# Encoder trunk: gate and up as seven quarter products per pair of tiles

## Chip, core and metric

The kernel runs on one core of one Trainium2 chip. The metric is the device time of one execution in microseconds, the median of several runs. Inside the program the engines run side by side, each with its own queue of instructions in order: TensorE (PE, with its weight loads PEld), VectorE (DVE), ScalarE (ACT), GpSimd (POOL), and SyncE (SP), which only issues transfers. They wait for each other through semaphores.

## What is computed

Two layers of an encoder trunk on 512 tokens of width 1024. Each layer has two feed-forward blocks, an attention mix of three branches, and a gated embedding. Cut to what matters here:

```python
def swiglu(x, w_gate, w_up, w_down):          # w_gate, w_up: 1024 x 2816, w_down: 2816 x 1024
    return (jax.nn.silu(x @ w_gate) * (x @ w_up)) @ w_down

for i in range(DEPTH):                        # DEPTH = 2
    h = h + 0.5 * swiglu(rms_norm(h, ffn1_norm[i]), ffn1_w_gate[i], ffn1_w_up[i], ffn1_w_down[i])
    ...                                       # three attention branches, merged through w_out
    h = h + 0.5 * swiglu(rms_norm(h, ffn2_norm[i]), ffn2_w_gate[i], ffn2_w_up[i], ffn2_w_down[i])
    h = h + jax.nn.sigmoid(rms_norm(h, ple_norm[i]) @ ple_w_gate[i]) * (p[i] @ ple_w_proj[i])
```

## The kernel before

The activations lie transposed: `h[d]` is a tile of 128 model rows by 512 tokens, d = 0 to 7. Everything is float32. A product is made exactly enough by splitting each operand into a rounded part `hi` (type fp32r) and the remainder `lo`, and adding three matmuls, hi x hi, lo x hi, hi x lo (`mm3`). Each matmul has a weight load of its own of 128x128.

The weights come from one DRAM tensor, `wall`, cut into chunks of 128 x 1024 in the order of use. `Weights.load` (L64) brings a chunk into `wraw` (four buffers) by a transfer on SP; `Weights.halve` makes `whi` on ACT (L75) and `wlo` on DVE, in the attention heads on POOL (L76), with three buffers each.

A feed-forward block is the function `ffn`. `Prep` has made the input parts `z[d]` (gain times `h[d]`, hi on ACT L328, lo on DVE L329); the norm's factor `rb` is applied after the product. For each of the 22 tiles `f` of 128 hidden rows: 24 matmuls for gate, 24 for up, each 512 tokens wide, then four operations on DVE and ACT and a split into `a[f]` (L175, L176). `down(g)` takes the hidden tiles of a group (two tiles, then five times four) through w_down: 8 output tiles, each added to `h[d]` on DVE (L371). It is written between the tiles `f`, one tile after the group is whole. `hooks` add small work after a given `f`: the bias tables of the first layer (`bias_vectors`, after f = 8) end in 24 transfers on POOL's queue (L253).

`mix` is the attention: 40 heads, whose matmuls are interleaved by a planner (`Filler`, with due times) with the projections that they need. All its 512-wide tiles, as those of `ffn`, come from one pool of `SLOTS` = 79 buffers (function `S`). `w_out` and `add_out` end it; `ple` is the embedding.

The program is written with tiles; a scheduler sets the order on each engine ahead of the run, so an instruction may stand earlier on its engine than the source has it if its inputs are there. Within an engine the order is then fixed.

```python
            else:
                run(proj(pg, W.get(gate), z))
                run(proj(pu, W.get(up), z))
            g1, u1 = S(f"{name}g1_{f}"), S(f"{name}u1_{f}")
            nc.vector.tensor_mul(g1, pg, rb)
            nc.scalar.activation(g1, g1, AF.Silu)
            nc.vector.tensor_mul(u1, pu, rb)
            nc.vector.tensor_mul(u1, u1, g1)
            a[f] = split(u1, f"{name}a{f}")
```

## Time and profile before

| | |
|---|---|
| median of 3 runs | 3021.95 us (3021.86 to 3022.31) |
| profiled execution: its time | 3021.52 us |
| its span, first to last instruction | 3019.7 us |
| granted TensorE clock | 0.998 |
| feed-forward blocks in the span, first to last matmul | 9.7 to 375.7, 1103.2 to 1463.3, 1507.5 to 1868.7, 2598.2 to 2958.3 us |

The span is 1.8 us shorter than the profiled execution's time. Sums are made against the span. A group of instructions is given by line, engine, operation and the tiles that it writes and reads (`out<-in`), with its count, busy time and mean duration. The duration of a matmul is a modelled end; the distance from start to start says what a row of matmuls costs. Tile names in the trace: `ffn20g` is the gate product of the second block of layer 0, `f_0` its input norm and `z` parts, `m0vc` the values of the third branch in layer 0.

### The profile page before, as it was taken

What the parts mean: (1) busy time and instruction counts of PE and PEld (TensorE: products, weight loads), DVE (VectorE), ACT (ScalarE), POOL (GpSimd) and SP (SyncE); (2) the same over time, 40 slices, a digit from 0 to 9 for tenths busy, and PEclk for the clock granted to TensorE, in tenths of its full rate; (3) what the DMA queues carried; (4) which work ended last, traced back from release to release, by engine and by line L of the source; (5) the groups of instructions that cost most, each with busy time, mean ns of one, the idle gap of its engine ahead of it and who ended that gap; (6) DMA issues with size and microseconds to landing.
All of it is one profiled execution on the core that took longest, in us unless ns stands there. A gap on an engine that the chain in (4) does not pass through costs nothing.

```text
span 3019.7 us, 37502 instructions
## 1 busy us (share of the span) xinstructions
PE 2966.6 (98%) x14206; PEld 2463.6 (82%) x14206; DVE 1837.0 (61%) x2844; ACT 1418.5 (47%) x2511; POOL 749.0 (25%) x709
## 2 busy tenths in 40 slices
PE   8999999999999999999999999999999999999998
PEld 7888878888878888888888888788888788888886
DVE  6444576646787765444664445866478877644446
ACT  4222356655677742223432223566467777422233
POOL 0010015444455530000200001144344555200003
PEclk9999999999999999999999999999999999999999
DMA  4363332122222233333333334211222222333332
GB/s 154 99 221 98 122 126 70 49 70 73 77 77 79 76 116 98 97 93 97 125 103 95 96 98 158 83 63 57 63 82 74 68 75 75 124 95 96 98 98 91
DMA packets 81525, 287.75 MB, mean 95 GB/s; under 512 B 10382, under 2 KB 12430, under 8 KB 81344
## 3 DMA queue, kind: packets, MB, share of 16 engines
q1 hardware_dynamic: 66960, 240.42, 25.5%
q0 software_dynamic: 12080, 42.00, 4.1%
q10 hardware_dynamic: 2304, 2.94, 0.3%
q8 instruction: 111, 1.82, 0.2%
q14 instruction: 70, 0.57, 0.1%
HBM read 274.76 MB, written 18.94 MB: 97 GB/s over the span
## 4 chain that ended last, share of the span: by engine, by line
PE 88%; DVE 6%; ACT 4%; issue 2%; POOL 0%; DMA 0%; ACTq 0%; DVEq 0%; POOLq 0%
PE ffn10g L165 4%; PE ffn10u L165 4%; PE ffn21g L165 4%; PE ffn20g L165 4%; PE ffn21u L165 4%; PE ffn20u L165 4%; PE ffn21d L165 4%; PE ffn11d L165 4%; PE ffn10d L165 4%; PE ffn20d L165 4%; PE ffn11g L165 4%; PE ffn11u L165 4%; PE wo L165 3%; PE ple L165 3%; PE m1ga L165 1%
## 5 line engine op out<-in xcount | busy, mean ns | idle before, releaser
L75 ACT CAST whi<-wraw 128x1024 fp32r<-128x1024 f32 x456 | 478.4, 1052 | 1057.0 <-issue 371.3
L76 DVE TENSOR_TENSOR wlo<-wraw,whi 128x1024 fp32r<-128x1024 f32 x312 | 383.6, 1232 | 124.3 <-ACT whi L75 124.0
L76 POOL TENSOR_TENSOR wlo<-wraw,whi 128x1024 fp32r<-128x1024 f32 x144 | 353.4, 2457 | 366.5 <-ACT whi L75 322.0
L287 POOL TENSOR_TENSOR pg0sq<-pg0sq,pg0sq 128x512 f32<-128x512 f32 x7 | 11.1, 1586 | 345.0 <-ACT pg0sq L282 345.0
L287 POOL TENSOR_TENSOR pg1sq<-pg1sq,pg1sq 128x512 f32<-128x512 f32 x7 | 11.1, 1583 | 345.1 <-ACT pg1sq L282 345.1
L419 POOL DMA_DIRECT2D h_dram<-wo0h x8 | 4.3, 541 | 341.2 <-DVE wo0h L371 341.2
L371 DVE SCALAR_TENSOR_TENSOR wo0h<-ffn11d,wo0h 128x512 f32<-128x512 f32 x48 | 32.8, 689 | 40.9 <-PE ffn11d L165 40.9
L371 DVE SCALAR_TENSOR_TENSOR x<-ffn10d,x 128x512 f32<-128x512 f32 x48 | 32.8, 689 | 40.9 <-PE ffn10d L165 40.9
L371 DVE SCALAR_TENSOR_TENSOR wo1h<-ffn21d,wo1h 128x512 f32<-128x512 f32 x48 | 32.8, 689 | 38.7 <-PE ffn21d L165 38.7
L371 DVE SCALAR_TENSOR_TENSOR wo0h<-ffn20d,wo0h 128x512 f32<-128x512 f32 x48 | 32.8, 689 | 38.7 <-PE ffn20d L165 38.7
L388 DVE TENSOR_TENSOR ffn20u<-ffn20u,f_0r 128x512 f32<-128x512 f32 x22 | 15.2, 691 | 62.0 <-PE ffn20u L165 62.0
L388 DVE TENSOR_TENSOR ffn21u<-ffn21u,f_1r 128x512 f32<-128x512 f32 x22 | 15.2, 691 | 62.0 <-PE ffn21u L165 62.0
L388 DVE TENSOR_TENSOR ffn10u<-ffn10u,f_0r 128x512 f32<-128x512 f32 x22 | 15.2, 691 | 59.8 <-PE ffn10u L165 59.8
L419 POOL DMA_DIRECT2D h_dram<-x x8 | 4.3, 540 | 189.1 <-DVE x L371 189.1
L388 DVE TENSOR_TENSOR ffn11u<-ffn11u,f_1r 128x512 f32<-128x512 f32 x22 | 15.2, 691 | 59.2 <-PE ffn11u L165 59.2
L386 DVE TENSOR_TENSOR ffn21g<-ffn21g,f_1r 128x512 f32<-128x512 f32 x22 | 15.2, 691 | 47.0 <-PE ffn21g L165 46.9
L386 DVE TENSOR_TENSOR ffn20g<-ffn20g,f_0r 128x512 f32<-128x512 f32 x22 | 15.2, 691 | 47.0 <-PE ffn20g L165 46.9
L386 DVE TENSOR_TENSOR ffn10g<-ffn10g,f_0r 128x512 f32<-128x512 f32 x22 | 15.2, 691 | 44.5 <-PE ffn10g L165 44.4
L386 DVE TENSOR_TENSOR ffn11g<-ffn11g,f_1r 128x512 f32<-128x512 f32 x22 | 15.2, 690 | 44.1 <-PE ffn11g L165 44.1
L248 POOL DMA_DIRECT2D bias_s<-bvs x1 | 0.5, 519 | 142.5 <-DVE bvs L246 142.5
L287 POOL TENSOR_TENSOR f_1sq<-f_1sq,f_1sq 128x512 f32<-128x512 f32 x14 | 21.0, 1500 | 58.5 <-ACT f_1sq L282 58.3
L598 ACT CAST m0kc<-m0kc 64x512 fp32r<-64x512 f32 x32 | 18.6, 580 | 13.7 <-PE m0kc L165 6.1
(5072 smaller groups left out, 10383.7 us busy)
## 6 DMA issues: line engine op xcount, KB each, us to landing
wraw<-in_wall SPq DMA_DIRECT2D x456, 512.0 KB, 3.5
copies_s<-bias_s POOLq DMA_DIRECT2D x16, 256.0 KB, 7.7
copies_d<-bias_d POOLq DMA_DIRECT2D x8, 512.0 KB, 15.1
h_dram<-x POOLq DMA_DIRECT2D x8, 256.0 KB, 2.7
pp_dram<-m0ppt POOLq DMA_DIRECT2D x8, 256.0 KB, 4.7
wo0h<-h_dram POOLq DMA_DIRECT2D x8, 256.0 KB, 5.3
ple0p<-pp_dram POOLq DMA_DIRECT2D x8, 256.0 KB, 4.9
h_dram<-wo0h POOLq DMA_DIRECT2D x8, 256.0 KB, 2.7
```

What stands on the lines that cost most here:

```text
L75: self.nc.scalar.copy(hi, raw)
L76: self.lo_engine.tensor_tensor(lo, raw, hi.bitcast(F32), op=ALU.subtract)
L165: nc.tensor.matmul(ps, lhsT, rhs, start=start, stop=stop, skip_group_check=True)
L248: nc.gpsimd.dma_start(bias_s, bv[0:n, :])
L287: self.engine.tensor_tensor(self.acc, self.acc, sq, op=ALU.add)
L371: nc.vector.scalar_tensor_tensor(h[d], ps, 0.5, h[d], op0=ALU.mult, op1=ALU.add)
L386: nc.vector.tensor_mul(g1, pg, rb)
L388: nc.vector.tensor_mul(u1, pu, rb)
L419: nc.gpsimd.dma_start(h_dram[d], h[d])
L598: nc.scalar.copy(ks[e][r], ps[own])
```

## The change

From the second pair of hidden tiles on (p = 1 to 10 of 11), gate and up of a pair are each computed as a 2x2 block product: the two hidden tiles give two blocks of weight columns, the 1024 model rows two blocks of 512, and the 512 tokens two halves of 256 (`A`, `B`). Instead of eight quarter products there are seven, of four `mm3` each, 256 tokens wide, after the scheme of Strassen and Winograd.

- `Combos` makes the four sums of input quarters from `h`, once per block, in the time of the first pair, which is still done the plain way.
- `Quad` is one pair's gate or up. Its weights are two chunks, loaded on SP into `X` and `Y`, and half of the second again into `Z`. Two of the four sums of weights are made by transfers that add to their destination (on POOL's queue, `accum_op`), one by POOL and one by DVE (`took`).
- Two PSUM tiles, `R` and `V`, hold the partial products; copies on ACT and sums on DVE form the two results `t1`, `t2`. The last product (4) of a pair is done within the next pair.
- The factor `rb` enters through the gate: after Silu, POOL multiplies it in again, so that up needs no factor.
- Splitting into hi and lo goes by halves of 512 columns; two halves share a tile pair. A fourth tile pair is in a pool of its own.
- The steps of a block stand in a list, and `prepare` runs splits ahead of them by `AHEAD` tiles, loads by `LOADS` steps. `down` groups follow pairs 1, 3, 5, 7; the last two groups come at the end.
- Memory: the common pool has 62 buffers. The space of the other 17 and of the strips is a pool that is opened for each stage: weights' tiles in the feed-forward blocks, 17 tiles (`kept`) and the strips in `mix`.
- The second half of `w_out` goes column by column, so that `h[4]` to `h[7]` are done one after the other. The number of matmuls is the same.

```diff
+PAIRS = FT // 2
+DOWN_AFTER = {1: 0, 3: 1, 5: 2, 7: 3}
...
+    def tiles(self, stage=None):
+        n = self.pairs
+        self.pairs += 1
+        if stage is not None and n % 4 == 3:
+            return tuple(stage.tile([P, 1024], F32R, tag=f"w{x}2", name=f"w{x}{n}", bufs=1) for x in ("hi", "lo"))
+        return tuple(self.pool.tile([P, 1024], F32R, tag=f"w{x}", name=f"w{x}{n}", bufs=3) for x in ("hi", "lo"))
+    def part(self, hi, lo, raw):
+        self.nc.scalar.copy(hi, raw)
+        self.lo_engine.tensor_tensor(lo, raw, hi.bitcast(F32), op=ALU.subtract)
...
+    def open_stage(for_weights):
+        guard = tc.tile_pool(name=f"stage{len(stages)}", bufs=1, reuse_waits="tile")
+        pool = guard.__enter__()
+        stages.append(guard)
+        W.stage = pool if for_weights else None
+        return pool
...
+    class Combos(Prep):
+        def quarters(self):
+            A, B = HALVES
+            z = self.z
+            self.q = {1: [[t[:, A] for t in z[k]] for k in range(4)], 2: [[t[:, A] for t in z[4 + k]] for k in range(4)],
+                      3: [[t[:, B] for t in z[4 + k]] for k in range(4)], 4: [None] * 4, 5: [None] * 4, 6: [None] * 4, 7: [None] * 4}
+        def combine(self, k):
+            A, B = HALVES
+            name, one, two = self.name, self.at + k, self.at + 4 + k
+            zf = S(f"{name}zf{k}")
+            nc.scalar.activation(zf, h[k], AF.Copy, scale=col(self.l, one))
+            first, second = S(f"{name}t57{k}"), S(f"{name}t64{k}")
+            gain, other = col(self.l, two), ncol(self.l, two)
+            lo, hi = h[4 + k][:, A], h[4 + k][:, B]
+            nc.vector.tensor_sub(first[:, A], zf[:, A], zf[:, B])
+            nc.vector.scalar_tensor_tensor(second[:, A], hi, other, first[:, A], op0=ALU.mult, op1=ALU.subtract)
+            nc.vector.scalar_tensor_tensor(first[:, B], hi, gain, zf[:, B], op0=ALU.mult, op1=ALU.subtract)
+            nc.vector.scalar_tensor_tensor(second[:, B], lo, other, second[:, A], op0=ALU.mult, op1=ALU.subtract)
+            for t, nm, ops in ((first, "t57", (5, 7)), (second, "t64", (6, 4))):
+                parts = split(t, f"{name}{nm}{k}")
+                for i, c in zip(ops, HALVES):
+                    self.q[i][k] = [x[:, c] for x in parts]
...
+        def load(self):
+            L, R = slice(0, 512), slice(512, 1024)
+            n, m = self.places
+            stage, wall = W.stage, ins["wall"]
+            if self.weight.endswith("gate"):
+                X = stage.tile([P, 1024], F32, tag="wx", name=f"{self.name}x", bufs=2)
+            else:
+                X = wpool.tile([P, 1024], F32, tag="wraw", name=f"{self.name}x", bufs=4)
+            Y = stage.tile([P, 1024], F32, tag="wy", name=f"{self.name}y", bufs=4)
+            Z = stage.tile([P, 512], F32, tag="wz", name=f"{self.name}z", bufs=4)
+            nc.sync.dma_start(Y, wall[m])
+            nc.sync.dma_start(X, wall[n])
+            nc.sync.dma_start(Z, wall[m][:, L])
+            nc.gpsimd.dma_start(Y[:, L], wall[m][:, R], accum_op=ALU.add)
+            nc.gpsimd.dma_start(Z, wall[n][:, L], accum_op=ALU.add)
+            self.X, self.Y = X, Y
+            self.source = {1: X[:, L], 2: X[:, R], 5: Y[:, L], 6: X[:, L], 3: X[:, R], 7: Z, 4: Y[:, R]}
+        def took(self, i):
+            L, R = slice(0, 512), slice(512, 1024)
+            if i == 1:
+                nc.gpsimd.tensor_tensor(self.X[:, L], self.X[:, L], self.Y[:, L], op=ALU.add)
+            elif i == 2:
+                nc.vector.tensor_add(self.X[:, R], self.X[:, R], self.X[:, L])
+        def product(self, i, w):
+            A, B = HALVES
+            if i == 1:
+                self.R = PS(f"{self.name}R", "s")[:, A]
+                self.t = S(f"{self.name}t1"), S(f"{self.name}t2")
+            elif i == 2:
+                self.V = PS(f"{self.name}V", "a")
+            ps = {2: lambda: self.V[:, A], 5: lambda: self.V[:, B], 3: lambda: self.V[:, B]}.get(i, lambda: self.R)()
+            wh, wl = w
+            for k in range(4):
+                c = slice(k * P, (k + 1) * P)
+                zh, zl = self.combos.q[i][k]
+                mm3(ps, wh[:, c], wl[:, c], zh, zl, i in (1, 2) and k == 0, i in (4, 3) and k == 3)
+            t1, t2 = self.t
+            if i == 1:
+                nc.scalar.copy(t1[:, A], self.R)
+            elif i == 5:
+                nc.scalar.copy(t2[:, A], self.V[:, B])
+            elif i == 6:
+                nc.scalar.copy(t1[:, B], self.R)
+            elif i == 3:
+                nc.vector.tensor_add(t1, self.V, t1)
+            elif i == 7:
+                nc.vector.tensor_add(t2[:, B], self.R, t2[:, A])
...
+        def plain_pair():
+            for f in range(2):
+                pg, pu = PS(f"{name}g{f}"), PS(f"{name}u{f}")
+                gate, up = ("cols", tag + "_w_gate", l, f), ("cols", tag + "_w_up", l, f)
+                if f == 0:
+                    together((pg, pu), W.get(gate, up), prep.z)
+                    rstd()
+                    prep.quarters()
+                else:
+                    run(proj(pg, W.get(gate), prep.z))
+                    run(proj(pu, W.get(up), prep.z))
+                g1, u1 = S(f"{name}g1_{f}"), S(f"{name}u1_{f}")
+                nc.vector.tensor_mul(g1, pg, rb[0])
+                nc.scalar.activation(g1, g1, AF.Silu)
+                nc.vector.tensor_mul(u1, pu, rb[0])
+                nc.vector.tensor_mul(u1, u1, g1)
+                a[f] = split(u1, f"{name}a{f}")
+                for k in (2 * f, 2 * f + 1):
+                    prep.combine(k)
...
-                run(proj(pg, W.get(gate), z))
-                run(proj(pu, W.get(up), z))
-            g1, u1 = S(f"{name}g1_{f}"), S(f"{name}u1_{f}")
-            nc.vector.tensor_mul(g1, pg, rb)
-            nc.scalar.activation(g1, g1, AF.Silu)
-            nc.vector.tensor_mul(u1, pu, rb)
-            nc.vector.tensor_mul(u1, u1, g1)
-            a[f] = split(u1, f"{name}a{f}")
-            for g, fs in enumerate(GROUPS[:-2]):
-                if f == fs[-1] + 1:
-                    down(g)
-            if f in hooks:
-                hooks[f]()
-        root_table()
...
+        def gate_half(q, n):
+            t, r = q.t[n], rb[0]
+            if n == 0:
+                nc.vector.tensor_mul(t, t, r)
             else:
+                nc.vector.scalar_tensor_tensor(t[:, B], t[:, B], -1.0, r[:, B], op0=ALU.mult, op1=ALU.mult)
+                nc.vector.scalar_tensor_tensor(t[:, A], q.R, -1.0, r[:, A], op0=ALU.mult, op1=ALU.mult)
+            nc.scalar.activation(t, t, AF.Silu)
+            nc.gpsimd.tensor_tensor(t, t, r, op=ALU.mult)
+        def up_half(q, gq, n, f):
+            t, g = q.t[n], gq.t[n]
+            if n == 0:
+                nc.vector.tensor_mul(t, t, g)
+            else:
+                nc.vector.scalar_tensor_tensor(t[:, B], t[:, B], -1.0, g[:, B], op0=ALU.mult, op1=ALU.mult)
+                nc.vector.scalar_tensor_tensor(t[:, A], q.R, -1.0, g[:, A], op0=ALU.mult, op1=ALU.mult)
+            a[f] = split(t, f"{name}a{f}")
+        def product(q, i, then=lambda: None):
+            def do(w):
+                q.product(i, w)
+                then()
+            steps.append(("product", (q, i), do))
+        tail = []
+        for p in range(1, PAIRS):
+            G, U = [Quad(f"{name}{x}{p}", tag + "_w_" + w, p, prep) for x, w in (("g", "gate"), ("u", "up"))]
+            for i in (1, 2):
+                product(G, i)
+                product(U, i)
+            for fn in tail:
+                fn()
+            for i in (5, 6, 3, 7):
+                product(G, i, (lambda G=G: gate_half(G, 0)) if i == 3 else lambda: None)
+                product(U, i, (lambda G=G, U=U, p=p: up_half(U, G, 0, 2 * p)) if i == 3 else lambda: None)
+            tail = [lambda G=G: product(G, 4, lambda: gate_half(G, 1)),
+                    lambda G=G, U=U, p=p: product(U, 4, lambda: up_half(U, G, 1, 2 * p + 1))]
+            if p in DOWN_AFTER:
+                down(DOWN_AFTER[p])
+        at = len(steps)
         down(len(GROUPS) - 2)
+        for k, fn in enumerate(tail):
+            fn()
+            steps.insert(at + 2 + k, steps.pop())
         down(len(GROUPS) - 1, True)
+        plain_pair()
...
+        def load_upto(n):
+            while state["loaded"] < min(n, len(steps)):
+                kind, what, _ = steps[state["loaded"]]
+                if kind == "down":
+                    W.load(base[what] + 1)
+                elif what[0].source is None:
+                    what[0].load()
+                state["loaded"] += 1
+        def prepare():
+            n = state["n"]
+            kind, what, _ = steps[n]
+            load_upto(n + LOADS)
+            if kind == "down":
+                place = base[what]
+                W.load(place + 1)
+                hi, lo = W.tiles(stage)
+                W.part(hi, lo, W.raw.pop(place))
+                ready[n] = (hi, lo), state["tiles"]
+                state["tiles"] += 1
+                W.split = max(W.split, place + 1)
+            else:
+                if state["half"] is None:
+                    state["half"] = W.tiles(stage), state["tiles"]
+                    state["tiles"] += 1
+                    c, (tiles, no) = slice(0, 512), state["half"]
+                else:
+                    c, (tiles, no) = slice(512, 1024), state["half"]
+                    state["half"] = None
+                q, i = what
+                W.part(tiles[0][:, c], tiles[1][:, c], q.source[i])
+                q.took(i)
+                ready[n] = tuple(t[:, c] for t in tiles), no
+            state["n"] += 1
...
+        hooked = set()
+        for n, (kind, what, do) in enumerate(steps):
+            while n not in ready:
+                prepare()
+            w, no = ready.pop(n)
+            while state["n"] < len(steps) and state["tiles"] - no <= AHEAD:
+                prepare()
+            if state["n"] == len(steps):
+                W.halve(len(W.keys) + AHEAD - (state["tiles"] - 1 - no))
+                W.load(len(W.keys) + AHEAD + 1)
+            do(w)
+            if kind == "product" and what[1] == 3 and what[0].weight.endswith("up"):
+                for f in (2 * what[0].p, 2 * what[0].p + 1):
+                    if f in hooks and f not in hooked:
+                        hooked.add(f)
+                        hooks[f]()
+            if n == len(steps) - 7:
+                root_table()
...
+        stage = open_stage(False)
+        def kept(nm, dt=F32):
+            return stage.tile([P, 512], dt, tag="kept", name=f"{name}{nm}", bufs=17)
...
+            if half == 1:
+                d = 4 + kk
+                sums[d] = PS(f"{name}{d}")
+                yield from proj(sums[d], W.get(("cols", "w_out", l, d)), m)
+                return
...
-            if d == 4:
-                for gen in outs:
-                    run(gen)
+            if d >= 4:
+                run(outs[d - 4])
...
-SLOTS = 79
+AHEAD = 2
+SLOTS = 62
+LOADS = 18
```

More of the change, by code (lines that the diff above doesn't have):

```diff
@@ L186, in encoder_kernel @@
         nc.scalar.dma_start(h[d], ins["xT"][d * P:(d + 1) * P, :])
+    nsmall = const.tile([P, L * 8], F32, name="nsmall")
     ones_r = const.tile([P, P], F32R, name="ones")
@@ L195, in encoder_kernel @@
     nc.gpsimd.memset(eps, 1e-6)
+    for l in range(L):
+        for i, at in enumerate((S_F1, S_F2)):
+            s = slice(l * 8 + 4 * i, l * 8 + 4 * i + 4)
+            nc.gpsimd.tensor_scalar(nsmall[:, s], small[:, l * S_N + at + 4:l * S_N + at + 8], -1.0, 1.0, op0=ALU.mult, op1=ALU.mult)
     perm = const.tile([64, P], F32, name="perm")
@@ L397, in ffn @@
+        at = len(steps)
         down(len(GROUPS) - 2)
+        for k, fn in enumerate(tail):
+            fn()
+            steps.insert(at + 2 + k, steps.pop())
         down(len(GROUPS) - 1, True)
+        plain_pair()
+        quads = []
+        for kind, what, _ in steps:
+            if kind == "product" and what[0] not in quads:
+                quads.append(what[0])
+        order = []
+        for kind, what, _ in steps:
+            if kind == "down":
+                order.append(("down", what))
+            elif what[0].places is None:
+                q = what[0]
+                q.places = ()
+                order.append(("quad", q))
@@ L440, in mix @@
         h.clear()
-        trig = [S(f"{name}trig{i}") for i in range(3)]
+        trig = [kept(f"trig{i}") for i in range(3)]
         for i in range(3):
```

133 lines of the change are left out of this document (88 added, 45 removed).

## Prediction

> **What bounds the kernel now.** I read the page's heads first, then the order of starts on TensorE, then the stages by windows, then VectorE and GpSimd where their work collides.
>
> ```profile
> span 3019.7 us, 37502 instructions
> PE 2966.6 (98%) x14206; PEld 2463.6 (82%) x14206; DVE 1837.0 (61%) x2844; ACT 1418.5 (47%) x2511; POOL 749.0 (25%) x709
> PE   8999999999999999999999999999999999999998
> POOL 0010015444455530000200001144344555200003
> PE 88%; DVE 6%; ACT 4%; issue 2%; POOL 0%; DMA 0%; ACTq 0%; DVEq 0%; POOLq 0%
> ```
>
> TensorE is busy in every slice and is 88% of the chain that ended last. POOL is nearly idle in the feed-forward blocks (its zeros and ones). The busy share says nothing of what one matmul costs, so I take starts from the timeline: start, duration, engine and line.
>
> ```profile
> 1212.89 0.39 PE L165 MATMUL ffn20g<-f_0z0h,whi 128*128 128x512 f32 x1
> 1256.41 0.39 PE L165 MATMUL ffn20d<-ffn20a6h,whi 128*128 128x512 f32 x1
> 681.15 0.28 PE L165 MATMUL m0vc<-whi,m0u0h 128*128 128x256 f32 x1
> 689.67 0.28 PE L165 MATMUL m0vc<-wlo,m0u7h 128*128 128x256 f32 x1
> 681.16:689.70 8.54, 8.54 (x72) 8.54 (x71) 0.85 (x2) 0.75 (x2) 1.00 0.20 63
> ```
>
> Between the first two rows lie two hidden-tile pairs of gate and up, 192 matmuls of 512 columns: 43.52 us, 226.7 ns each. The other two are the first and last of 72 matmuls of 256 columns in attention: 71 steps in 8.52 us, 120.0 ns each. The last row is that window's sum for these instructions alone (PE, then its weight loads): every matmul has its own load. So two halves cost 240 ns where one whole costs 226.7; a product of 7/8 the work saves 7.3%, not 12.5%.
>
> **The change part by part.**
>
> *Matmuls.* A pair's gate and up are now 96 x 226.7 = 21.76 us. After: 2 x 7 x 12 = 168 matmuls x 120.0 = 20.16 us. Saved 1.60 us a pair; 40 pairs (10 in each of 4 blocks) give 64.0 us. At 119.7 ns it would be 66; an added wait of 1.60 us a pair takes all of it.
>
> *VectorE's own work.* The rows are groups of block `ffn20` (1110 to 1458 us: count, busy, mean ns), three starts in a row, and the 256-wide form.
>
> ```profile
> L76 DVE TENSOR_TENSOR wlo<-wraw,whi 128x1024 fp32r<-128x1024 f32 x64 | 78.2, 1223 | 20.4 <-ACT whi L75 20.4
> L371 DVE SCALAR_TENSOR_TENSOR wo0h<-ffn20d,wo0h 128x512 f32<-128x512 f32 x46 | 31.5, 689 | 38.4 <-PE ffn20d L165 38.4
> 1224.77 0.69 DVE L389 TENSOR_TENSOR ffn20u<-ffn20u,ffn20g 128x512 f32<-128x512 f32 x1
> 1225.38 1.22 DVE L76 TENSOR_TENSOR wlo<-wraw,whi 128x1024 fp32r<-128x1024 f32 x1
> 1226.52 0.68 DVE L176 TENSOR_TENSOR ffn20a7l<-ffn20u,ffn20a7h 128x512 fp32r<-128x512 f32 x1
> L521 DVE TENSOR_TENSOR m0va<-m0va,m0va x16: 406/424/425, 447.8 to 572.1; 128x256 fp32r<-128x256 f32 x16
> 1217.00:1260.40 43.40, 43.40 (x193) 35.95 (x192) 20.71 (x25) 13.05 (x16) 0.00 (x0) 1.00 0.29 96
> ```
>
> Back to back, 512 columns cost 0.61 us and 1024 cost 1.14; a 256-wide one, 0.42 long, about 0.34 by the same overlap. Now two pairs take 20.71 us of VectorE in 43.4. After, a pair has 14 lo halves, 2 `took`, 2 sums of `V`, gate and up scaling, 2 splits: 22 of 512 and 6 of 256, 22 x 0.61 + 6 x 0.34 = 15.5 us in 20.16. It fits.
>
> *VectorE against POOL.* New on POOL in the blocks: per pair two `took` sums and two multiplications by `rb`, 512 wide. Where POOL ran beside VectorE, the trace has this:
>
> ```profile
> 1085.10 5.37 POOL L287 TENSOR_TENSOR f_0sq<-f_0sq,f_0sq 128x512 f32<-128x512 f32 x3 [2.71 <-ACT f_0sq L282]
> 1087.55 1.78 DVE L329 SCALAR_TENSOR_TENSOR f_0z1l<-wo0h,small,f_0z1h 128x512 fp32r<-128x512 f32 x1
> 1090.95 0.74 DVE L329 SCALAR_TENSOR_TENSOR f_0z3l<-wo0h,small,f_0z3h 128x512 fp32r<-128x512 f32 x1
> L836 POOL TENSOR_TENSOR m0C1sql<-m0C1sq,m0C1sqh x1: 1290/1290/1290, 785.3 to 785.3; 128x512 fp32r<-128x512 f32 x1
> ```
>
> A VectorE operation on two SBUF tiles takes 1.78 us beside POOL's sums and 0.74 after them; POOL's take 5.37/3 = 1.79 there and 1.29 undisturbed. They take turns. One collision as seen costs VectorE 1.04 us; with all four colliding once a pair is 15.5 + 4.2 = 19.7 us, under 20.16 with little left. If each POOL sum shuts it out for all of its undisturbed 1.29, it is 20.7. The Trainium skill, SBUF — State Buffer, section Who interferes with whom, has this as an exclusive lock for the whole instruction, between a VectorE operation with two SBUF inputs and a GpSimd operation that reads SBUF; by it the sum would be 20.7, over TensorE's. I take 19.7, the collisions as measured. A `down` of 96 matmuls lasts 21.8 us and needs 8 x 0.61 + 4 x 1.14 = 9.4 of VectorE, so it gives slack; it follows every second pair, and only pairs 8, 9 and 10 stand in a row. The lead of three split tiles is six products, 8.6 us. VectorE's order on them is fixed, and a gate that POOL returns late holds all lo halves behind it: I take 2.5 us at each block's end, 10 in all; the ends are 0 and 30 (0.75 a pair).
>
> *ScalarE.*
>
> ```profile
> L175 ACT CAST ffn20a2h<-ffn20u 128x512 fp32r<-128x512 f32 x1 | 0.6, 626 | 0.4 <-DVE ffn20u L389 0.4
> L520 ACT CAST m0va<-m0va x16: 361/372/431, 446.2 to 571.7; 128x256 fp32r<-128x256 f32 x16
> ```
>
> A pair: 14 halves, 2 Silu, 2 hi of `a`, 18 x 0.63, and 6 PSUM copies x 0.37: 13.6 us in 20.16. Hidden; if late, TensorE waits at products 5 to 7, which come three products (4.3 us) after the copy's source.
>
> *The start of a block.* `combine` adds per block sixteen 256-wide and eight 512-wide VectorE operations (10.3 us), ScalarE 12 x 0.63 = 7.6. Product 5 needs them 5.8 us after the plain pair. With six lo halves and two `took` for two whole splits, VectorE gets 10.3 + 3.7 + 1.2 - 2.3 = 12.9 us more.
>
> ```profile
> 35.34 0.39 PE L165 MATMUL ffn10g<-f_0z0h,whi 128*128 128x512 f32 x1
> 10.00:37.00 27.00, 27.00 (x106) 21.32 (x106) 23.44 (x29) 19.29 (x27) 0.00 (x0) 1.00 0.50 187
> 1083.00:1131.00 48.00, 48.00 (x211) 39.39 (x210) 34.47 (x31) 22.81 (x31) 12.12 (x7) 1.00 0.39 122
> 1463.00:1507.00 44.00, 44.00 (x194) 36.09 (x193) 27.28 (x32) 19.99 (x27) 11.08 (x13) 1.00 0.45 140
> ```
>
> The first row is the third tile's start: the plain pair ends at 35.3. The others' columns are stretch, length, PE, PEld, DVE, ACT, POOL, clock, DMA share, GB/s. First block: 23.4 + 12.9 = 36.3 us of VectorE for 31 (10 to 35.3 + 5.8): 5 late. Both `ffn2`: 34.5 + 12.9 = 47.4 in 48, full; 2 each. Second `ffn1`: 16.7 us idle just before, nothing. Together 9; ends 0 and 25 (12.9 in the first, 4 in each other).
>
> *Transfers.*
>
> ```profile
> wraw<-in_wall SPq DMA_DIRECT2D x456, 512.0 KB, 3.5
> copies_s<-bias_s POOLq DMA_DIRECT2D x16, 256.0 KB, 7.7
> copies_d<-bias_d POOLq DMA_DIRECT2D x8, 512.0 KB, 15.1
> wo0h<-h_dram POOLq DMA_DIRECT2D x8, 256.0 KB, 5.3
> q0 software_dynamic: 12080, 42.00, 4.1%
> 10.00:15.00 5.00, 5.00 (x12) 3.48 (x12) 5.00 (x7) 4.62 (x7) 0.00 (x0) 1.00 1.03 380
> ```
>
> A pair loads 3.5 MB with the accumulated halves, against 2 before; without `down` that is 174 GB/s, and 380 was reached. No row shows a transfer that adds. Its landing lies between 3.5 us (a plain load) and 15.1 (the slowest on POOL's queue); nearest is 5.3, a load of the same 256 KB on that queue, and I take that. `Y` frees about a pair (20 us) before its next user needs the sum: 3.5 + 5.3 fits, 3.5 + 15.1 just. Priced at 0, hidden by that pair; if not, product 5 waits. But the adding transfer waits on POOL for the plain load to land; behind it stand `took` and the gate's multiplication, and behind that VectorE's `up_half` with all lo halves. SP issues three loads in place of two, in order: one that waits for its buffer holds those behind it, covered by the same 20 us.
>
> *One place where POOL is stuck already:*
>
> ```profile
> 152.16 4.72 POOL L253 DMA_DIRECT2D copies_s<-bias_s  x9 [2.01 <-DMA bias_s<-bvs]
> 174.17 0.52 POOL L253 DMA_DIRECT2D copies_d<-bias_d  x1 [1.97 <-DMA copies_s<-bias_s]
> 150.00:184.00 34.00, 34.00 (x152) 28.15 (x151) 15.89 (x19) 8.63 (x10) 14.85 (x29) 1.00 0.90 299
> ```
>
> An issue takes POOL 4.72/9 = 0.52 us, so a pair is 4 x 1.79 + 4 x 0.52 = 9.2 us of POOL. The 24 bias copies hold its queue for 22.5 us (152.16 to 174.69), mostly waiting, with transfers at 90%. Nothing needed POOL then; now each gate does. Cost between 0 and 22.5 - 8.6 (the lead) = 14, once. I take 5.
>
> *Edits at nothing.* `nsmall`: four tiny POOL operations before the first matmul. `w_out` by columns: 24 matmuls a chunk as before, `h[4]` to `h[6]` earlier. The 62 + 17 buffers: `kept` can make a fourth key set wait for the first.
>
> ```profile
> L600 DVE TENSOR_TENSOR m0kc3l<-m0kc,m0kc x4: 682/688/696, 711.3 to 714.7; 64x512 fp32r<-64x512 f32 x4
> L165 PE MATMUL m0C0s<-m0kc0l,m0qc x8: 389/389/389, 714.0 to 721.2; 128*128 128x512 f32 x8
> ```
>
> Set 3 is written by 714.7 while set 0 is read until 721.2; 15 buffers hold three sets of four, so one tile waits 6 us, needed only at 784. Zero; at worst 6 a layer, 12.
>
> **Sum.** 3019.7 - 64.0 + 10 + 9 + 5 = 2979.7 us of span. The profiled execution took 1.8 us more than its span, the median 0.4 more than that execution: 2982 us. The ends: all stalls zero, 2958; all at their upper ends (30 + 25 + 14 + 12), 3039.
>
> **Rivals.**
>
> *All stalls hidden:* the six products of lead and the free quarter of VectorE cover everything. For it: the trace before shows no wait of TensorE within a block. Against: VectorE's 47.4 of 48 at the starts. Time 2958.
>
> *The lock binds:* every pair runs at 20.7 to 21.2 us, because POOL's sums shut VectorE out whole and themselves stretch by 0.5 (1.79 less 1.29). For it the 1.78 against 0.74; against it the slack under `down`. 40 x 0.8 = 32 us in place of 10: 3004 with the other terms, 3000 to 3014.
>
> *Slower: POOL's queue binds.* If each of four adding transfers holds POOL until its plain load has landed, a pair needs 4 x (3.5 + 0.52) + 4 x 1.79 = 23.2 us on POOL, 3.1 more than TensorE's 20.16. It decides from 21.76 a pair on; at 23.2 the time is 2958 + 123 = 3081, at 22.3 3044. For it: queues are in order. Against: loads are issued 18 steps (26 us) ahead.
>
> *The matmul is not cheaper:* the weight loads, 188 ns long each, are not hidden behind 256 columns, and a pair costs 168 x 0.188 = 31.6 us: 3019.7 + 393 = 3413.
>
> ```profile
> L165 PEld LDWEIGHTS m0C0s<-m0kc0l,m0qc x8: 187/188/188, 713.8 to 721.0; 128*128 128x128 f32 x8
> ```
>
> Against it: 120.0 ns with 71 loads in the same window. The Trainium skill, TensorE: Matmul & The Clock Gate, section Back-to-back issue gap, sets the pace of load and matmul together, about 81 ns at 128 columns and 131 at 512; an estimate between them for 256 is 98, by which 168 cost 3.9 us more than 96. The trace disagrees with both figures here.
>
> **Chances.** Forecast, 2967 to 2998: 0.50. All hidden, 2956 to 2967: 0.18. Lock, 2998 to 3016: 0.18. POOL's queue, over 3016: 0.13. Loads: 0.01. The range 2958 to 3014 leaves out the queue, the loads and a few per cent at both ends, 0.2 in all; the forecast's own is 2967 to 2998. Within 0.2% (6 us, about what a measurement of this kernel can tell from no change) lie the lightest queue case and the heaviest lock: 0.05. Faster 0.84, slower 0.11.
>
> **What would show it.** TensorE: 14206 + 40 x 72 = 17086 matmuls, 256-wide ones in the blocks 120 ns apart. VectorE at three quarters or more in pairs without `down`, and lo halves of 0.69 us stretched to over 1.2 beside POOL. Waits of TensorE at product 5 of pair 1, and in the first block between 150 and 185 us. Queue q0 near 84 MB (42 and 160 adding transfers of 0.26). Wrong would be: waits spread over every pair that end on POOL or a transfer; starts further apart than 120 ns without a wait; or new waits in the attention stage.

## The result, and the profile after

| | before | after |
|---|---|---|
| median | 3022.05 us (4 runs) | 3044.44 us (3043.26 to 3045.66, 4 runs) |
| ratio, with its 95% interval | | 1.0074 (1.0057 to 1.0092) |
| profiled execution, its span | 3021.52, 3019.7 us | 3043.61, 3041.8 us |
| granted TensorE clock | 0.998 | 0.986 |

The changed kernel is 0.7% slower; 2982 us was forecast, with a range that ended at 3014. First the head of its page: TensorE's matmuls, the three other engines, the granted clock by slices, and the chain that ended last.

```profile
span 3041.8 us, 45943 instructions
PE 2930.9 (96%) x17086; PEld 2566.1 (84%) x17086; DVE 2158.9 (71%) x3580; ACT 1666.8 (55%) x3201; POOL 1114.2 (37%) x1033
PE   7989999999999998999989999999999999899997
PEclk8999999999999999999989999999999999999999
PE 76%; DVE 11%; ACT 5%; issue 4%; DMA 3%; POOL 1%; ACTq 0%; DVEq 0%; SPq 0%; POOLq 0%
```

The count is the forecast's 17086, and TensorE's busy time did fall by 36 us. But the chain now holds 11% of VectorE where it held 6%, and PE's row has eights in slices that were nines: TensorE waits. Where, the view of waits says (engine and line, what it waited for: us in all, times, longest), here those of the feed-forward blocks over 2.5 us, without the wait for the first input at the program's start:

```profile
PE ffn10d L218 <- ACT ffn10a9h L229: 9.6, 1, 9.6
PE ffn20g1V L218 <- ACT f_0t572h L229: 5.5, 1, 5.5
PE ffn21g1V L218 <- ACT f_1t572h L229: 5.5, 1, 5.5
PE ffn10g1V L218 <- ACT f_0t572h L229: 5.2, 1, 5.2
PE ffn11g1V L218 <- ACT f_1t572h L229: 5.2, 1, 5.2
PE ffn10g3R L218 <- ACT ffn10g3t L499: 3.2, 1, 3.2
PE ffn11g1V L218 <- ACT f_1t571h L229: 2.7, 1, 2.7
```

`t57` are the operand sums for products 5 and 7; the last digit is k, `h` the rounded part. Each of the four blocks waits at product 5 of pair 1 for the sum k = 2; the first block waits besides for `a[9]` and in its pair 3. In block `ffn20` this looks so (windows: stretch, length, PE, PEld, DVE, ACT, POOL busy, clock, DMA share, GB/s):

```profile
1131.80:1156.20 24.40, 24.40 (x130) 20.82 (x130) 17.06 (x26) 13.81 (x21) 4.43 (x3) 1.00 0.13 45
1156.20:1170.00 13.80, 5.38 (x26) 4.33 (x25) 12.77 (x25) 7.88 (x14) 1.74 (x2) 0.70 0.56 153
1398.00:1438.30 40.30, 39.98 (x333) 39.78 (x332) 33.99 (x54) 22.40 (x45) 13.71 (x13) 1.00 0.67 184
```

The first stretch is from the last `h` to product 5: TensorE full, VectorE idle for 7.3 us. In the second, product 5 of gate and up takes 13.8 us in place of 2.9. The third is two pairs in a row later in the block: TensorE full at 120 ns a matmul, VectorE at 17.0 us a pair. So the pairs run as hoped and the blocks' starts do not. From a block's first matmul to its last, by starts in the timeline, in us:

| | ffn10 | ffn20 | ffn11 | ffn21 |
|---|---|---|---|---|
| before | 365.6 | 359.7 | 360.8 | 359.7 |
| after | 388.1 | 358.2 | 362.9 | 356.3 |
| after, no_sums (below) | 373.5 | 346.2 | 347.6 | 345.2 |

Ten pairs of 1.6 us should have taken 16 from each block. They lost 38.5, 14.5, 18.1 and 12.6 us against that: 83.7 in all, against 64.0 saved, and 2.4 us more outside the blocks: together the 22.1 us by which the span grew.

A part of the loss is the clock. Windows around pair 3 of the first block, and at that block's product 5:

```profile
113.00:117.30 4.30, 1.14 (x10) 1.02 (x9) 2.11 (x9) 1.92 (x5) 1.02 (x1) 1.00 0.79 198
117.31:120.72 3.41, 3.41 (x18) 3.41 (x17) 2.16 (x4) 3.20 (x7) 0.00 (x0) 0.50 0.62 190
45.63:62.70 17.07, 8.60 (x34) 7.57 (x35) 14.14 (x26) 9.33 (x18) 1.73 (x2) 0.50 0.48 123
```

Another such stretch ends at 171.93. The timeline has two neighbouring 256-column matmuls in it, and two after its end:

```profile
168.55 0.41 PE L218 MATMUL ffn10g4R<-f_0t570h,wlo 128*128 128x256 f32 x1
168.76 0.41 PE L218 MATMUL ffn10g4R<-f_0t570l,whi 128*128 128x256 f32 x1
172.43 0.28 PE L218 MATMUL ffn10u4R<-f_0t573h,whi 128*128 128x256 f32 x1
172.54 0.28 PE L218 MATMUL ffn10u4R<-f_0t573h,wlo 128*128 128x256 f32 x1
```

After the wait of 3.2 us in the first row the granted clock is 0.50 for 3.41 us; around product 5, where waits follow each other, for 17.07. Starts are then 0.21 us apart in place of 0.12. Counted over the trace, some 170 matmuls of the blocks start so late, 16.9 us in all; before, 13 with 2.3. The Trainium skill, TensorE: Matmul & The Clock Gate, section What's actually happening, has a free-running window of 3.4 us, with half the clock after an idle one. The lengths agree: the stretches here last 3.41, 10.24 and 17.07 us, one, three and five such windows. The condition fits less well: the wait of 3.2 us is shorter than a window.

### The profile page after: what moved, and what is told of

Same layout as the page of the kernel before. It is cut to its first block, busy times and chain, and to the rows that moved or that the text cites. A ratio compares the mean times of both kernels' runs of the same rounds, so it can differ in the third digit from the quotient of the medians.

```text
span 3041.8 us, 45943 instructions
## 1 busy us (share of the span) xinstructions
PE 2930.9 (96%) x17086; PEld 2566.1 (84%) x17086; DVE 2158.9 (71%) x3580; ACT 1666.8 (55%) x3201; POOL 1114.2 (37%) x1033
## 3 DMA queue, kind: packets, MB, share of 16 engines
q0 software_dynamic: 35120, 83.95, 12.6%
## 4 chain that ended last, share of the span: by engine, by line
PE 76%; DVE 11%; ACT 5%; issue 4%; DMA 3%; POOL 1%; ACTq 0%; DVEq 0%; SPq 0%; POOLq 0%
PE ffn21d L218 4%; PE ffn11d L218 4%; PE ffn10d L218 4%; PE ffn20d L218 4%; PE ple L218 3%; DVE wlo L101 2%; PE m0ga L218 1%; PE m1ga L218 1%; PE m0gb L218 1%; PE m1gb L218 1%; PE m0vc L218 1%; PE m1vc L218 1%; PE m0qc L218 1%; PE m0kc L218 1%; PE m1qb L218 1%
## 5 line engine op out<-in xcount | busy, mean ns | idle before, releaser
L100 ACT CAST whi<-wraw 128x1024 fp32r<-128x1024 f32 x296 | 310.5, 1051 | 212.5 <-issue 60.4
L101 DVE TENSOR_TENSOR wlo<-wraw,whi 128x1024 fp32r<-128x1024 f32 x152 | 189.9, 1252 | 93.3 <-ACT whi L100 92.9
L894 ACT CAST m1kc<-m1kc 64x512 fp32r<-64x512 f32 x32 | 18.6, 582 | 18.5 <-PE m1kc L218 15.2
L847 DVE SCALAR_TENSOR_TENSOR m1qc<-m1qc,m1qc 64x512 fp32r<-64x512 f32 x16 | 11.0, 688 | 20.0 <-ACT m1qc L846 19.9
L847 DVE SCALAR_TENSOR_TENSOR m0qc<-m0qc,m0qc 64x512 fp32r<-64x512 f32 x16 | 11.0, 688 | 20.0 <-ACT m0qc L846 19.9
L846 ACT ACTIVATE m1qc<-m1qc 64x512 fp32r<-64x512 f32 x16 | 9.5, 594 | 21.4 <-PE m1qc L218 13.2
L846 ACT ACTIVATE m0qc<-m0qc 64x512 fp32r<-64x512 f32 x16 | 9.5, 593 | 21.4 <-PE m0qc L218 13.2
L1313 POOL TENSOR_SCALAR out<-wo1h,small 128x512 f32<-128x512 f32 (+1 forms) x9 | 7.2, 795 | 33.0 <-DVE wo1h L1277 33.0
L915 DVE TENSOR_TENSOR m1vc<-m1vc,m1vc 128x256 fp32r<-128x256 f32 x16 | 6.4, 414 | 13.3 <-ACT m1vc L914 13.1
L847 DVE SCALAR_TENSOR_TENSOR m1qb<-m1qb,m1qb 64x512 fp32r<-64x512 f32 x16 | 11.0, 688 | 4.8 <-ACT m1qb L846 4.5
```

The costliest lines, as they stand in the source:

```text
L100: self.nc.scalar.copy(hi, raw)
L101: self.lo_engine.tensor_tensor(lo, raw, hi.bitcast(F32), op=ALU.subtract)
L846: nc.scalar.activation(qs[e][own], ps[own], AF.Copy, scale=-0.125)
L847: nc.vector.scalar_tensor_tensor(qs[e][other], ps[own], -0.125, qs[e][own].bitcast(F32), op0=ALU.mult, op1=ALU.subtract)
L894: nc.scalar.copy(ks[e][r], ps[own])
L915: nc.vector.tensor_sub(t[:, 256:512], ps, t[:, 0:256].bitcast(F32))
```

## The experiments

The expectations name the theories: A, the place of the operand sums in the queues; B, VectorE's amount of work; C, late transfers; D, a chain from tile to tile; E, ScalarE; F, amount and place together; G, the products' need of the sums; H, the norm's root. The medians, and the ratio to the kernel before, run on the same chip beside each. The kernel before took 3021.6 to 3022.7 us in these measurements, and single executions of a changed one lie up to 11 us apart, so that 2 or 3 us between two rows say nothing:

| run | median, us | ratio (95%) |
|---|---|---|
| no_sums | 2992.7 | 0.9902 (0.9885 to 0.9918) |
| early_sums | 3042.6 | 1.0066 (1.0051 to 1.0081) |
| rescale_later | 3046.9 | 1.0076 (1.0061 to 1.0091) |
| sums_split | 3052.4 | 1.0096 (1.0081 to 1.0111) |
| root_first | 3045.2 | 1.0074 (1.0059 to 1.0089) |
| sums_no_lo | 3037.3 | 1.0050 (1.0035 to 1.0065) |
| early_no_lo | 3024.3 | 1.0009 (1.0000 to 1.0018) |
| sums_fill_v | 3015.6 | 0.9981 (0.9972 to 0.9991) |
| sums_fill_s | 2999.7 | 0.9930 (0.9913 to 0.9947) |
| copies_late | 3035.4 | 1.0038 (1.0023 to 1.0053) |
| hooks_out | 3035.6 | 1.0044 (1.0029 to 1.0059) |
| queues_free | 3028.2 | 1.0019 (1.0010 to 1.0029) |
| sums_split_queues | 3034.8 | 1.0045 (1.0031 to 1.0059) |
| two_plain | 3012.9 | 0.9971 (0.9962 to 0.9981) |
| two_plain_queues | 2993.6 | 0.9905 (0.9891 to 0.9920) |
| two_plain_late_tile | 3010.3 | 0.9964 (0.9951 to 0.9977) |
| two_plain_in_order | 2985.6 | 0.9877 (0.9861 to 0.9894) |

**The price of the operand sums.** `no_sums`:

```diff
+            self.q[5] = self.q[7] = [[t[:, B] for t in z[k]] for k in range(4)]
+            self.q[4] = self.q[6] = self.q[3]
...
-                for k in (2 * f, 2 * f + 1):
-                    prep.combine(k)
```

> Leaves out the operand sums: products 4 to 7 read plain quarters of z that are there already, so gate and up of all tiles from the third on are other numbers. It prices the whole step. Theory A and rival B both expect the start of a block without waits of over 1 us and a granted clock of 1.0 in ffn20: 3044 - 62 = 2982 us (2976 to 2988). Rival C (the first pair's adding transfers or their halves are late, and the sums only look like it): waits stay at products 5 to 7 of pair 1 and the time stays over 3005 us.

Measured 2992.7, above the 2976 to 2988 that A and B gave: the sums cost 52 us and not 62, or by the table of blocks 14.6, 12.0, 15.3 and 11.1. Theory C is out. In that kernel's `ffn20` the first stretch goes from the last `h` to product 5, the second is the 14 us from there:

```profile
1117.50:1142.00 24.50, 24.50 (x130) 20.89 (x129) 17.13 (x24) 13.39 (x21) 4.45 (x3) 1.00 0.13 43
1142.00:1156.00 14.00, 14.00 (x109) 13.59 (x109) 9.58 (x12) 7.45 (x13) 4.56 (x4) 1.00 0.81 224
```

VectorE has 7.4 us free before product 5, where the sums are 10.3, and 4.4 after it.

**The place of the sums: four orders, no gain.** The timeline of the changed kernel points to the order (VectorE, ScalarE and the rescaling of the second plain tile):

```profile
1130.09 0.68 DVE L1246 SCALAR_TENSOR_TENSOR wo0h<-wo,wo0h 128x512 f32<-128x512 f32 x1
1131.82 0.74 DVE L393 SCALAR_TENSOR_TENSOR f_0z7l<-wo0h,small,f_0z7h 128x512 fp32r<-128x512 f32 x1
1139.29 1.23 DVE L101 TENSOR_TENSOR wlo<-wraw,whi 128x1024 fp32r<-128x1024 f32 x1 [6.73 <-ACT whi L100]
1151.18 0.72 ACT L433 ACTIVATE f_0zf<-wo0h,small 128x512 f32<-128x512 f32 x1
1160.61 0.69 DVE L553 TENSOR_TENSOR ffn20g<-ffn20g,f_0r 128x512 f32<-128x512 f32 x1
1164.86 0.62 ACT L229 CAST f_0t572h<-f_0t 128x512 fp32r<-128x512 f32 x1 [0.89 <-DVE f_0t L439]
```

`h[7]` is final at 1130.8 (first row), VectorE idles 6.73 us, and the first sum starts at 1151.18; k = 2 stands behind the second tile's rescaling. `early_sums`:

```diff
                     together((pg, pu), W.get(gate, up), prep.z)
+                    prep.quarters()
+                    for k in range(4):
+                        prep.combine(k)
                     rstd()
-                    prep.quarters()
...
-                for k in (2 * f, 2 * f + 1):
-                    prep.combine(k)
```

> All four operand sums of a block (the helper combine, k = 0 to 3) are emitted right behind the matmuls of the first hidden tile and ahead of its rescaling, in place of two behind each of the first two tiles; nothing else differs from the changed kernel. Theory A (place): the sums are late because they stand behind other work in VectorE's and ScalarE's queues; then the waits at product 5 of pair 1 (13.8 us in block ffn20, about 62 us over the four blocks, with the halved clock in them) fall to 3 us or less each and the time to 2992 us (2985 to 3003). Rival B (amount): VectorE has no room for 12.9 us more at a block's start wherever they stand; then the waits move to the first two tiles' own splits or rescaling and the time stays above 3028 us.

3042.6: no gain in all. `ffn20` and `ffn21` became 4.7 and 6.1 us shorter, `ffn11` stayed, `ffn10` became 6.1 longer; new waits stand in both `ffn1` blocks:

```profile
PE ffn10g1V L218 <- ACT f_0r L372: 15.2, 1, 15.2
PE ffn11g1V L218 <- ACT f_1r L372: 9.4, 1, 9.4
```

The norm's root, `f_0r`, is now behind the sums on ScalarE. In `ffn20`, from the first sum to the second tile's split, VectorE is busy for 33.26 us of 33.60:

```profile
1138.90:1172.50 33.60, 28.95 (x154) 24.32 (x153) 33.26 (x49) 21.80 (x36) 4.07 (x3) 0.97 0.23 78
```

`rescale_later` (only `combine(2)` and `combine(3)` ahead of the second tile's rescaling):

> The sums k = 2 and 3 are emitted ahead of the second plain tile's rescaling in place of behind it; nothing else differs from the changed kernel. Theory F (amount and place together: VectorE is full before product 5, so each microsecond of other work that stands ahead of a sum is a microsecond of TensorE's wait; the second tile's rescaling, first needed by the down projection 11 us later, stands there with a chain of 4.3 us from 1160.6 to 1164.9): 4 to 6 us a block with the shorter half clock, 3044 - 20 = 3024 us (3018 to 3030). Theory B (amount alone: what is moved behind is missed there): 3038 us or more.

3046.9, no gain. In `ffn20` the wait at k = 2 fell from 5.5 to 2.1 us, and the block is 0.6 us shorter: small waits came instead at k = 3 and in the down projection (1.2 us), and the stretch at half clock grew from 10.24 to 13.65 us. `sums_split` (the parts for products 5 and 7 behind the first tile's matmuls, the others behind the second's, each ahead of the rescaling):

> The same arithmetic in another order: of the four sums only the parts that products 5 and 7 read (5.4 us of VectorE) are made, right behind the first tile's matmuls and ahead of its rescaling; the parts for products 6 and 4 follow behind the second tile's matmuls and ahead of its rescaling. Theory F: the needless work ahead of product 5, 4.3 us of rescaling and 4 x 1.4 us of the other parts, goes from the path, some 10 of the 11 to 15 us a block: 3044 - 40 = 3004 us (2996 to 3014). Theory B: the waits go over to product 6 and to the products' own low halves, as where all sums stood first: 3030 us or more.

3052.4 in place of 3004. The longest waits of the blocks' starts are now for the rescaling itself, 8.1 us each in the two `ffn1` blocks, and for the root, 8.6 and 3.4:

```profile
PE ffn10g1V L218 <- ACT f_0r L372: 8.6, 1, 8.6
PE ffn11d L218 <- DVE ffn11g L565: 8.1, 1, 8.1
PE ffn10d L218 <- DVE ffn10g L565: 8.1, 1, 8.1
```

`root_first` (as `early_sums`, with `rstd()` ahead of the sums):

> As early_sums, but the norm's column sums, root and reciprocal are emitted ahead of the four operand sums. Theory H: in blocks ffn10 and ffn11 TensorE waited 15.2 and 9.4 us because ScalarE's root, which frees the PSUM bank that product 2 needs, stood behind the sums; with it first these waits go, the sums cost what VectorE's queue costs in ffn20 and ffn21 (some 7 us a block): 3043 - 20 = 3023 us (3016 to 3031). Theory B (VectorE's amount alone): the wait is only renamed, 3036 us or more.

3045.2 in place of 3023. The waits on the root are gone, as theory H has it, and the time stays. In the first block ScalarE stands for 6.2 us behind POOL, which makes a sum of weights behind its adding transfers, and most of the operand sums stand behind ScalarE's copy. The changed kernel has the same wait (third row), there ahead of all its operand sums.

```profile
26.69 0.71 ACT L433 ACTIVATE f_0zf<-x,small 128x512 f32<-128x512 f32 x1
33.60 0.62 ACT L100 CAST whi<-ffn10g1x 128x512 fp32r<-128x512 f32 x1 [6.20 <-POOL ffn10g1x L478]
33.66 0.62 ACT L100 CAST whi<-ffn10g1x 128x512 fp32r<-128x512 f32 x1 [6.08 <-POOL ffn10g1x L478]
```

So theories A, F and H fall: each order takes one wait away and meets the next within some us.

**Amount or need.** `sums_no_lo` leaves out the eight low halves, in the changed kernel's place; `early_no_lo` the same where the sums stand first:

```diff
-                parts = split(t, f"{name}{nm}{k}")
+                parts = S(f"{name}{nm}{k}h", F32R), self.z[k][1]
+                nc.scalar.copy(parts[0], t)
```

> Leaves out the eight low halves of the operand sums on VectorE (the low half of z stands in for each, so gate and up are other numbers); the sums themselves and ScalarE's work stay. Theory B (VectorE's amount): each of 8 x 0.61 = 4.9 us a block comes off the path, and some of the halved clock: 3044 - 22 = 3022 us (3016 to 3028). Rival E (ScalarE's zf and high halves in turn with VectorE set the pace): 3040 to 3046 us.

> All four sums first, as in early_sums, with their eight low halves left out (the low half of z in their place, so gate and up are other numbers). Theory B: 4.9 us less of VectorE's full queue a block, and less half clock: 3043 - 22 = 3021 us (3014 to 3028). Theory G: the chain through ScalarE stays as long, and the low halves are not in it: 3036 us or more.

7 us in the first place (between both theories), 18 us in the other (theory B's 22 within its bounds). This fits a chain from engine to engine that binds where the sums stand late, and VectorE's queue where they stand first. Then the amount alone, without need: `sums_fill_v` adds to `no_sums` VectorE's operations on tiles that nobody reads, `sums_fill_s` ScalarE's.

```diff
+            for i in range(4):
+                c = HALVES[i % 2]
+                nc.vector.tensor_sub(t[:, c], h[k][:, c], h[4 + k][:, c])
+            for i in range(2):
+                nc.vector.tensor_sub(t, h[k], h[4 + k])
```

> As no_sums (products 4 to 7 read plain quarters of z), but behind each plain tile VectorE gets the sums' own count and shapes of operations, 16 of 256 and 8 of 512 columns a block, on tiles that nothing reads; ScalarE gets nothing. Theory B (VectorE's amount in an ordered queue): most of the 52 us come back though nothing needs the result: 2993 + 42 = 3035 us (3025 to 3046). Theory G (the need: products 5 to 7 wait for a chain ScalarE, VectorE, ScalarE, VectorE): 2993 to 3002 us, since VectorE has 11.8 us idle in the 38.5 us from the last h to product 7 of that kernel.

> As no_sums, but behind each plain tile ScalarE gets the sums' own operations, 12 of 512 columns a block (7.6 us), on tiles that nothing reads; VectorE gets nothing. Theory B and theory G: 2993 to 2998 us. If ScalarE's queue binds at a block's start: 3008 us or more.

3015.6 and 2999.7: of the 52 us, VectorE's amount alone brings back 23, ScalarE's some 7. Neither theory's number came. In the first, product 5 of `ffn10` waits for a low half of its weights, which stands behind the fill:

```profile
PE ffn10g1V L218 <- DVE wlo L101: 7.2, 1, 7.2
```

The other 22 of the 52 us come only when the products need the sums; how they split between the chain and the two loads together stays open.

**The first block's queues.** `copies_late` moves the 24 bias copies, `hooks_out` also the table loads, constants and bias vectors, to seven steps before the block's end; `queues_free` is `copies_late` with the lambda loads issued a pair earlier than their arithmetic.

```diff
             if n == len(steps) - 7:
                 root_table()
+                if "end" in hooks:
+                    hooks["end"]()
```

> The 24 bias copies are emitted seven steps before the first block's end, behind the last multiplication of a gate by rb, in place of behind pair 4; the three small matmuls that make the bias vectors stay where they were. Theory: these copies held POOL's queue while the gate's multiplication for a[9] stood behind them; the 10.1 us wait of the down projection and the 2.2 us at half clock behind it go, nothing comes back later: 3044 - 12 = 3032 us (3028 to 3035). Rival: a[9] is late through the adding transfers on the same queue: within 3 us of 3044.

> As the run before, and the table loads, the constants and the bias vectors too are emitted there, in place of behind pairs 1, 2 and 4 of the first block. Theory: VectorE's queue stood behind the constants' transfers (3.3 us of waiting and 1.6 at half clock at 111 to 121 us) and behind the bias vectors (2.8, then 1.6 and 1.1 at 164 to 173 us); these 10 us go as well: 3022 us (3018 to 3027). Rival: the work returns at the start of the attention stage, where POOL is held by 24 copies: block ffn10 is 22 us shorter, but the stretch between it and ffn20 is longer by 5 us or more, 3027 us and above.

> As copies_late, and the two loads of the lambda vectors are issued with the tables behind pair 1, in place of with their arithmetic behind pair 2. Theory: VectorE's 3.9 us wait for the second of these loads held the low halves behind it, cost 3.3 us of TensorE and then 1.6 at half clock; both go: 3035 - 5 = 3030 us (3026 to 3033). Rival: ScalarE's table loads for Exp beside it (three of 1.28 us) hold the split as long: 3034 us or more.

The copies gave 9 of the expected 12 us; the wait for `ffn10a9h` is gone from the list. In the changed kernel the gate's multiplication stood behind them and one adding transfer on POOL (the last of the copies, and what follows):

```profile
200.79 0.52 POOL L317 DMA_DIRECT2D copies_d<-bias_d  x1 [0.93 <-DMA copies_s<-bias_s]
203.50 0.91 POOL L469 DMA_DIRECT2D ffn10u6y<-in_wall  x1 [2.19 <-issue]
204.11 1.59 POOL L570 TENSOR_TENSOR ffn10g4t<-ffn10g4t,f_0r 128x512 f32<-128x512 f32 x1
```

`hooks_out` gave nothing more in place of the 10 us expected: the bias matmuls now waited for tables that were loaded only then.

```profile
347.56 5.28 PE L308 MATMUL bv<-oh,tab 33*16 33x512 f32 x6 [5.00 <-DMA oh<-in_onehot]
```

Loading early and computing in place, `queues_free`, gave 16 us in all. With the split sums, `sums_split_queues`:

> The order of the run before, with the bias copies and the lambda loads placed as in queues_free, which was 16 us under the changed kernel. Theory F: 3004 - 16 = 2988 us (2980 to 2998), under the 2994 of the version with two plain pairs, which gives up 6.4 us of saving. Theory B: 3012 us or more.

3034.8 in place of 2988: 17.6 us off `sums_split`, so the queues' gain adds up, and theory F falls here too.

**More time for the sums.** `two_plain`: quarter products from the third pair on.

```diff
-        res += [p] * 4
+        res += [p if p > 1 else 0] * 4
...
-            for f in range(2):
+            for f in range(4):
...
-                for k in (2 * f, 2 * f + 1):
-                    prep.combine(k)
+                prep.combine(f)
...
-        for p in range(1, PAIRS):
+        down(0)
+        for p in range(2, PAIRS):
```

> The second pair of tiles is plain too: quarter products begin with pair 2, one operand sum stands behind each of the four plain tiles, and the first down projection comes before the first product. Per block this gives the sums 21.8 us more of matmuls (and 11.8 us of down) before product 5 and gives back 1.6 us of saving. Theory B (amount: VectorE had no room for the sums in the 24 us between the last h and product 5; no_sums priced that at 11 to 15 us a block, 53 in all): 3044 - 53 + 4 x 1.6 = 2997 us (2992 to 3003), no wait over 1 us at product 5 in blocks ffn20, ffn11 and ffn21. Rival D (the chain: each sum waits for the tile ahead of it in the queues, so that the last one is late wherever the sums stand): one sum in four still waited for, about 13 us of the 53 stay: 3010 us or more.

> Both edits of two_plain and of queues_free. Theory B with the queues: 2997 - 9 - 5 = 2983 us (2977 to 2990), 1.3% under the kernel before. Rival D: 2996 us or more. If the two edits overlap (the first block's waits hide one another), 2988 to 2995.

3012.9 and 2993.6, 16 and 11 us over what theory B gave; the first lies where theory D put it. The trace decides: no wait for an operand sum is left, as B says and D does not. What was missing: the copies' wait in `two_plain` (11.9 us), and in both a new one at the start of `ffn21`, behind this on ScalarE:

```profile
2559.76 0.71 ACT L398 ACTIVATE f_1z2h<-wo1h,small 128x512 fp32r<-128x512 f32 x1
2568.07 0.62 ACT L100 CAST whi<-ffn21u2y 128x512 fp32r<-128x512 f32 x1 [7.61 <-DMA ffn21u2y<-in_wall]
```

The scheduler had set a split of pair 2, whose weights an adding transfer still had to bring, ahead of the norm and `z` of the block that was about to start. `two_plain_late_tile` kept the free fourth tile from the block's first steps:

> As two_plain_queues, but the fourth split tile of a stage is used only from the ninth tile of a block's steps on. Theory: there a split of a quad's sum took that free tile at once, and ScalarE, in order, waited 7.6 us for its adding transfer at 2560 to 2568 us ahead of the next norm and z, which cost block ffn21 some 8 us at its start; without it 2993.6 - 8 = 2986 us (2982 to 2990). Rival: the start of ffn21 waits for h from memory whatever ScalarE does: 2992 us or more.

3010.3, a miss: another split (`ffn21g3x`, 6.0 us) came to the same place, and the first block, which had to start without that tile, is 10 us longer, with new waits for low halves of weights. `two_plain_in_order` holds those copies in program order instead:

```diff
+        op = self.nc.scalar.copy(hi, raw)
+        if held:
+            held(op)
...
+                W.part(..., tc.keep_in_program_order if n < 10 else None)
```

> As two_plain_queues, but ScalarE's copies of a block's first ten steps keep their place in the program's order, behind the norm and z. Theory: ScalarE no longer waits 5.6 and 7.6 us for adding transfers at 2549 to 2568 us, block ffn21 starts without its 8 us of waits and the stretches ahead of the ffn2 blocks lose some us too: 2993.6 - 10 = 2984 us (2980 to 2989). Rival: the first products now lack their split tiles and wait instead: 2993 us or more.

2985.6, within the expected 2980 to 2989, 1.2% under the kernel before, and the best of all. Lines of its page, and the window of `ffn20` with the fourth plain tile, the first down projection and the products up to 5:

```profile
PE 2919.1 (98%) x16798; PEld 2544.7 (85%) x16798; DVE 2130.7 (71%) x3516; ACT 1640.7 (55%) x3135; POOL 1082.5 (36%) x1001
PEclk9999999999999999999999999999999999999999
PE 83%; DVE 7%; ACT 4%; issue 4%; POOL 1%; DMA 0%; ACTq 0%; DVEq 0%; POOLq 0%
```

```profile
1129.00:1160.00 31.00, 31.00 (x171) 27.06 (x170) 28.08 (x46) 16.36 (x29) 3.53 (x2) 1.00 0.13 45
```

VectorE is nearly full there, 28.08 of 31.00 us, but TensorE is full as well: the same work, with 34 us more of matmuls ahead of its need.

## Why the prediction was wrong, step by step

- **Matmuls, -64.0 us: right.** Starts are 120 ns apart, and two pairs in a row take 40.3 us. The rival with weight loads not hidden is out.
- **VectorE against POOL, +10: next to nothing.** No wait at a block's end is over 0.5 us. VectorE has 17.0 us a pair, between the 15.5 without a collision and the 19.7 taken. No steady pair waits, so the lock's rival (3004) is out, and the queue's too, although the measured 3044 is its lower number. That is chance: by it a pair took 22.3 us, and in the three later blocks every pair from 2 to 9 without a `down` behind it takes 20.15, but for one of 21.05. Low halves beside POOL did stretch as forecast, one of 0.69 us to 2.48:

```profile
163.80 2.48 DVE L101 TENSOR_TENSOR wlo<-ffn10g5x,whi 128x512 fp32r<-128x512 f32 x1 [1.36 <-ACT whi L100]
```

- **The start of a block, +9: this is the step that failed.** It measured 52 (by the medians) to 53 us (by the blocks). The place was named (product 5 of pair 1), the size was not. The step filled 47.4 us of VectorE into 48 us of window and called it full. But that window reached 20 us ahead of the block. Its two halves, the second to 1132.90:

```profile
1083.00:1108.00 25.00, 25.00 (x112) 20.67 (x111) 17.80 (x17) 13.05 (x20) 9.32 (x6) 1.00 0.43 134
1108.50:1132.90 24.40, 24.40 (x108) 19.84 (x107) 17.14 (x17) 11.12 (x13) 2.30 (x2) 1.00 0.35 108
```

Half of VectorE's free time (7.2 us) lies ahead of 1108. The sums need `h[4]` to `h[7]`, which the changed kernel writes one by one, `h[4]` by 1116.9 and `h[7]` by 1130.8, 4.1 us after the block's first matmul (1.5 us in the kernel before). From 1112.70 to 1132.50 VectorE has no idle time there:

```profile
1112.70:1132.50 19.80, 19.02 (x83) 15.24 (x83) 19.80 (x18) 10.09 (x15) 11.16 (x11) 1.00 1.00 274
```

So only what is free later can be used: 7.4 us, for 10.3. In `no_sums` VectorE has 6.3, 6.8 and 5.8 us free up to product 5 in the other three blocks, from the last `h` on (in the first block from 9.00). And a bound by amount alone misses the hand-overs: each sum goes ScalarE, VectorE, ScalarE, VectorE, and the root, the rescaling and the halves stand between. For the second `ffn1` block the step said nothing late, because 16.7 us were free just before it; but its last `h`, too, comes 3.9 us after its first matmul, and it lost 15.3 on the sums. The upper end, 25, held 4 us for each later block, by the same windows, and so was no bound: they lost 11.1 to 15.3.
- **The clock was in no term.** Every wait was counted at its own length. Of the 83.7 us lost in the blocks, 14.6 are matmuls at half clock (16.9 less the 2.3 of before), nearly all behind waits; they are part of what the sums, the copies and the loads cost.
- **Bias copies, +5 (0 to 14):** 9 measured, within the ends. The lambda loads, 7 us by `queues_free` against `copies_late`, were not looked at: the step asked what holds POOL, not what holds VectorE's queue.
- **Transfers, 0: right for the steady pairs.** `no_sums` has no wait over 2.1 us at product 5. But the first block's copies on ScalarE stood 6.08 us behind POOL and its adding transfers; what this cost there no run took apart.
- **Buffers and `w_out`, 0: right.** The stretches between the blocks grew by 0.9 us at most.
- Sums, copies and lambda loads are 68 of the 83.7 us. The rest lies in waits of under 3 us each, with half clock behind some, that no run took apart.

## What to carry to other kernels

Count an engine's free time only from the moment at which the added work's last input exists to the moment at which its result is needed, not as a share of a stage. When the queue in that gap is full, another order only renames the wait; give the work more cover, even at the price of some of the saving (here 6.4 us of 64), and then clear the queues that it passes. Expect half clock behind a wait of TensorE of some 3 us: in these traces 3.41 us of it, which cost some 1.5 us more (16 starts 0.21 us apart in place of 0.12).
